# Norms at the end of a block: six layer norms on ScalarE and GpSimd, the rms scale on ScalarE, the rms norm's weights in the rows of the next projections

## The chip, the cores and the metric

The kernel runs on one core of a Trainium2 chip. The metric is the device time of one execution in microseconds. The engines are named as in the profile: PE (TensorE), DVE (VectorE), ACT (ScalarE), POOL (GpSimd) and SP, whose queue issues most DMAs.

## The reference

A sequence of 1024 tokens of width 1024 goes through a first block (layer norm, projection, an S5 state-space branch beside latent attention, a gated addition), a second block (rms norm, one wide projection, dilated attention beside a gated recurrence) and 32 experts. The change lies where the first block ends and the second begins. In the reference, in fp32:

```python
u = DEEPNORM_ALPHA * x + mix
ple = jax.nn.sigmoid(u @ w_pg[i]) * (p[i] @ w_pp[i])
x = layer_norm(u + ple, ln_g[i], ln_b[i])      # end of block 1, kept as x1
...
h = rmsnorm(x, norm1_g[layer])                 # start of block 2
z = h @ w_in[layer]                            # 3 x 512 + 4 x 512 columns
```

where `layer_norm` is (x - mean) * rsqrt(var + 1e-5) * g + b and `rmsnorm` is x * rsqrt(mean(x²) + 1e-6) * g, both over the 1024 columns.

## The kernel before

Tokens lie in 8 tiles `u[0..7]` of 128 tokens (partitions) by 1024 columns. Every fp32 product is made of three passes (`mm3`, L178 to L180): each operand is split into a rounded part h and a rest l, and PE sums h·h, h·l and l·h. A split (`split`) is one ACT operation for h (L146) and one DVE operation for l (L147).

Weights come in chunks (`Chunks`, `wload`): a chunk is 1024 rows by 256 columns, loaded in four pieces (kp 0 to 3) into `wraw` (two buffers) by SP, then split into `wh` and `wl` (eight buffers, so two chunks). `Chunks.next()` has the chunk after the present one issued as well. A piece of `wraw` comes free when its `wl` has been made.

A scheduler puts the instructions of each engine into one order when the program is built; each engine then takes its own row of instructions in that order, and waits where an operand isn't ready. That order, not the order in the code, says what stands behind a wait.

The stage in question is the last loop of `out_ple`. Per tile m, PE makes the last two quarters of the gate (60 matmuls of 256 columns), ACT takes the tanh (L695), DVE multiplies and adds it into u[m] (L696, L697). Then DVE takes the statistics and the reciprocal root (`ln_stats`, `rsqrt`: three Newton steps of small operations), applies the layer norm in two operations (L737, L738) with the gains `plg` and offsets `plb`, which are loaded as rows repeated on all partitions; SP stores the tile to `d_x1` (L739). `rms_transposed` lets ACT square and sum the tile (L751), DVE make the second root (L753 on) and scale the tile by root and gain `g1b` (L756), PE transpose it in eight 128x128 blocks (L215), and ACT and DVE evacuate and split the transposed tile into `aTh` and `aTl` (L146, L147), the operands of block 2.

Block 2 loads small constants (hmask, lb, hg), makes `lbt` on ACT (L1031), and begins its projections: `g_qk(0)` on tokens 0 to 511 (96 matmuls), `g_tok` on tiles 0 to 3 (96), `g_qk(0)` on tokens 512 to 1023 (96), `g_tok` on tiles 4 to 7 (96); after that, attention is woven between the other projections.

Of the kernel before, what the change touches and what calls it, by code (L numbers as in the profile page):

```python
# [11 lines left out]
FT = mybir.dt.float32  # L12
FR = mybir.dt.float32r
I32 = mybir.dt.int32
AF = mybir.ActivationFunctionType
OP = mybir.AluOpType
# [5 lines left out]
D = 1024  # L22
NT = 8
# [65 lines left out]
def bcast_rows(ap, n, parts=128):  # L89
    return bass.AP(tensor=ap.tensor, offset=ap.offset, ap=[[0, parts], [1, n]])  # L90


class Ctx:
# [58 lines left out]
                nc.scalar.activation(h, src, AF.Identity, scale=scale)  # L152
            nc.vector.scalar_tensor_tensor(l, src, scale, f32(h), op0=OP.mult, op1=OP.subtract)

    def wload(self, segs, nk, pj):

        nc = self.nc
        out = []
        n = sum(s.shape[1] for s in segs)
        for kp in range(nk // 2):  # L160
            raw = self.wp.tile([128, 2, WN], FT, name="wraw", bufs=2)
            o = 0
            for s in segs:
                w = s.shape[1]
                v = (s.rearrange("(p j) n -> p j n", j=nk) if pj
                     else s.rearrange("(j p) n -> p j n", p=128))
                nc.sync.dma_start(raw[:, :, o:o + w], v[:, 2 * kp:2 * kp + 2, :])
                o += w
            h = self.wp.tile([128, 2, WN], FR, name="wh")
            l = self.wp.tile([128, 2, WN], FR, name="wl")  # L170
            self.split(h[:, :, :n], l[:, :, :n], raw[:, :, :n])
            out += [(h[:, 0, :n], l[:, 0, :n]), (h[:, 1, :n], l[:, 1, :n])]
        return out

# [96 lines left out]
def block1(c):  # L271
# [111 lines left out]
    ym = [(yp.tile([128, S], FR, name=f"ymh{h}"), yp.tile([128, S], FR, name=f"yml{h}")) for h in range(4)]  # L383
    mla(c, ym, ess)
    out_ple(c, ym, esy)


# [5 lines left out]
def ln_stats(c, X):  # L393

    nc = c.nc
    n = len(X)
    mv = c.sm([128, n, 2], name="bmv")
    for i, x in enumerate(X):
        st = c.sm([128, 2, 6], name="bst")
        for h in range(2):  # L400
            nc.vector.bn_stats(st[:, h, :], x[:, h * 512:(h + 1) * 512])  # L401
        nc.vector.bn_aggr(mv[:, i], st)
    ve = c.sm([128, n], name="bve")
    nc.vector.tensor_scalar(ve, mv[:, :, 1], 1e-5, None, op0=OP.add)
    r = c.sm([128, n], name="brs")
    c.rsqrt(r, ve)
    mb = c.sm([128, n], name="bmb")
    nc.vector.scalar_tensor_tensor(mb, mv[:, :, 0], -1.0, r, op0=OP.mult, op1=OP.mult)
    return [(mv[:, i, 0:1], mb[:, i:i + 1], r[:, i:i + 1]) for i in range(n)]
# [224 lines left out]
def out_ple(c, ym, esy):  # L634
    tc, nc, I = c.tc, c.nc, c.I
# [14 lines left out]
    ch = Chunks(c, [([I["w_out"][:, s]], 8, False) for s in ns] + [([I["w_pg"][:, s]], 8, True) for s in ns])  # L650
# [10 lines left out]
    for n in range(4):  # L661
        w = ch.next()
        for m in range(NT):
# [3 lines left out]
            if n == 3:  # L667
                if m % 2 == 0:
                    uT.append(alloc_aT())
                js = slice((m % 2) * 128, (m % 2) * 128 + 128)  # L670
                c.transpose8(u[m], True, lambda q: tuple(a[:, 4 * q:4 * q + 4, js] for a in uT[m // 2]))
    esy.close()
    q = c.pool(es, "ple")
# [10 lines left out]
    def gate(m, w):  # L684
        js = slice((m % 2) * 128, (m % 2) * 128 + 128)
        psa = c.ps((128, 256))
        c.gemm(psa, [(tuple(a[:, k, js] for a in uT[m // 2]), w[k]) for k in range(8)])
        return psa

    def add(m, n, psa):  # L690
        ms = slice(m * 128, (m + 1) * 128)
        psb = c.ps((128, 256))
        c.gemm(psb, [((pTh[:, k, ms], pTl[:, k, ms]), (wph[:, k, ns[n]], wpl[:, k, ns[n]])) for k in range(2)])
        th = q.tile([128, 256], FT, name="th", bufs=2)
        nc.scalar.activation(th, psa, AF.Tanh, scale=0.5)  # L695
        nc.vector.scalar_tensor_tensor(th, th, 1.0, psb, op0=OP.add, op1=OP.mult)  # L696
        nc.vector.tensor_tensor(u[m][:, ns[n]], u[m][:, ns[n]], th, op=OP.add)  # L697
# [3 lines left out]
    for m2 in range(4):  # L701
        ps = c.psum_tile("T", [128, 2, 2, 128])
        for i in range(2):
            m = 2 * m2 + i
# [15 lines left out]
                add(m, n, gate(m, w))  # L720
    g_b = q.tile([128, D], FT, name="plg")
    b_b = q.tile([128, D], FT, name="plb")
    g1 = q.tile([128, D], FT, name="g1b")
    nc.sync.dma_start(g_b, bcast_rows(I["ln_g"], D))
    nc.sync.dma_start(b_b, bcast_rows(I["ln_b"], D))
    nc.sync.dma_start(g1, bcast_rows(I["norm1_g_2"], D))
    w = ch.next(), ch.next()
    for m in range(NT):
        add(m, 2, gate(m, w[0]))
        add(m, 3, gate(m, w[1]))  # L730
        if m % 2 == 0:
            c.hT.append(alloc_aT())
        x = u[m]
        ms = slice(m * 128, (m + 1) * 128)
        c.dbg("u_ple", x, lambda o: o[ms, :])
        (mean, _, r), = ln_stats(c, [x])
        nc.vector.scalar_tensor_tensor(x, x, mean, g_b, op0=OP.subtract, op1=OP.mult)  # L737
        nc.vector.scalar_tensor_tensor(x, x, r, b_b, op0=OP.mult, op1=OP.add)  # L738
        nc.sync.dma_start(d_x1[ms, :], x)  # L739
        c.dbg("x1", x, lambda o: o[ms, :])  # L740
        js = slice((m % 2) * 128, (m % 2) * 128 + 128)
        rms_transposed(c, q, x, [a[:, :, js] for a in c.hT[m // 2]], g1)
    es.close()


def rms_transposed(c, q, x, dst, g):

    nc = c.nc
    ss = c.sm([128, 1], name="rss")
    junk = q.tile([128, D], FT, name="junk")  # L750
    nc.scalar.activation(junk, x, AF.Square, accum_out=ss)  # L751
    v = c.sm([128, 1], name="rv")
    nc.vector.tensor_scalar(v, ss, 1.0 / D, 1e-6, op0=OP.mult, op1=OP.add)  # L753
    r = c.sm([128, 1], name="rr")
    c.rsqrt(r, v)
    nc.vector.scalar_tensor_tensor(x, x, r, g, op0=OP.mult, op1=OP.mult)  # L756
    c.transpose8(x, True, lambda h: tuple(a[:, 4 * h:4 * h + 4] for a in dst))


def s5_prep(c, es):  # L760
# [252 lines left out]
def block2(c):  # L1013

    tc, nc, I = c.tc, c.nc, c.I
# [5 lines left out]
    k = c.pool(es, "b2k")  # L1021
# [12 lines left out]
    nc.vector.tensor_scalar(fc[:, 1], th, 0.25, 0.75, op0=OP.mult, op1=OP.add)  # L1034
    nc.vector.tensor_scalar(fc[:, 2], th, 0.25, -0.25, op0=OP.mult, op1=OP.add)
    c.oss = k.tile([128, S], FT, name="oss")
    fp = c.pool(es, "b2f")
    tok = lambda kk, m: tuple(a[:, kk, (m % 2) * 128:(m % 2) * 128 + 128] for a in c.hT[m // 2])
    two = lambda kk, mm: tuple(a[:, kk, :] for a in c.hT[mm])
    bs = lambda o, b, n=1: W[:, o + b * 128:o + (b + n) * 128]  # L1040
    ft = lambda n, dt=FT: fp.tile([128, S], dt, name=n, tag="f", bufs=8)
    QK, V, G, FQ = {}, {}, {}, {}
    ch = Chunks(c, [([s], 8, True) if not isinstance(s, tuple) else (list(s), 8, True) for s in (
        (bs(0, 0), bs(512, 0)), bs(1024, 0, 2), (bs(0, 1), bs(512, 1)), (bs(0, 2), bs(512, 2)), bs(1024, 2, 2),
        (bs(0, 3), bs(512, 3)), bs(2560, 0, 2), (bs(2048, 0), bs(1536, 0)), bs(3072, 0, 2),
        (bs(2048, 1), bs(1536, 1)), bs(3072, 2, 2), (bs(2048, 2), bs(1536, 2)), bs(2560, 2, 2),
# [104 lines left out]
    r = c.con.tile([128, NT], FT, name="arr")  # L1151
# [769 lines left out]
def build(tc, I, out, dbg=None):  # L1921
    c = Ctx(tc, I, dbg)
    block1(c)
    rt = block2(c)
    c.es_ps.close()
    c.esw.close()
    moe(c, rt, out)
    c.es_ps.close()
    c.es_x2.close()
    c.es.close()  # L1930
# [37 lines left out]
```

## Time and profile before

| what | value |
|---|---|
| median of 3 runs | 2118.91 us (2117.28 to 2119.07) |
| the profiled execution's own time | 2121.21 us |
| its span | 2119.4 us, mean granted PE clock 0.954 |
| PE busy | 1937.4 us (91%) |
| DVE busy | 1549.3 us (73%) |
| ACT busy | 1031.9 us (49%) |
| POOL busy | 359.6 us (17%) |
| last loop of `out_ple` | 704.0 to 763.8 us (last gate matmul) |
| first four projection groups of block 2 | end at 827.1 us |

Times in the profile are counted from the start of the span. Busy time of PE is the time in which matmuls were in flight. A row of waits names the engine and line that waited, what it waited for, the total, the number of waits and the longest. The granted clock is 1.00 at full speed and 0.50 when PE is throttled.

### The profile page before, as it was taken

What the parts mean: (1) busy time and instruction counts of PE and PEld (TensorE: products, weight loads), DVE (VectorE), ACT (ScalarE), POOL (GpSimd) and SP (SyncE); (2) the same over time, 40 slices, a digit from 0 to 9 for tenths busy, and PEclk for the clock granted to TensorE, in tenths of its full rate; (3) what the DMA queues carried; (4) which work ended last, traced back from release to release, by engine and by line L of the source; (5) the groups of instructions that cost most, each with busy time, mean ns of one, the idle gap of its engine ahead of it and who ended that gap; (6) DMA issues with size and microseconds to landing.
All of it is one profiled execution on the core that took longest, in us unless ns stands there. A gap on an engine that the chain in (4) does not pass through costs nothing.

```text
span 2119.4 us, 34707 instructions
## 1 busy us (share of the span) xinstructions
PE 1937.4 (91%) x13274; PEld 1719.4 (81%) x13274; DVE 1549.3 (73%) x2974; ACT 1031.9 (49%) x1572; POOL 359.6 (17%) x265
## 2 busy tenths in 40 slices
PE   3997987799999979999999999999799999999992
PEld 2785875588999979899999898898688888888881
DVE  7878887777334795766457455658999999999995
ACT  3323334344222234545333223235688888888883
POOL 3124333300000000010010000003322222222211
PEclk9998998799999989999999998899899999999996
DMA  4444443311313131111111010456899999999984
GB/s 172 131 130 136 126 121 108 94 37 36 140 41 110 51 108 47 49 51 46 48 43 47 26 36 27 147 196 235 289 370 377 380 369 373 366 367 360 358 306 170
DMA packets 145081, 350.74 MB, mean 165 GB/s; under 512 B 33568, under 2 KB 87456, under 8 KB 120336
## 3 DMA queue, kind: packets, MB, share of 16 engines
q1 hardware_dynamic: 129632, 327.48, 43.0%
q0 software_dynamic: 10384, 17.87, 3.4%
q10 hardware_dynamic: 4896, 3.15, 0.7%
q8 instruction: 105, 1.72, 0.3%
q14 instruction: 64, 0.52, 0.1%
HBM read 305.81 MB, written 56.11 MB: 171 GB/s over the span
## 4 chain that ended last, share of the span: by engine, by line
PE 47%; issue 25%; DVE 14%; POOL 6%; DMA 3%; ACT 2%; SPq 1%; POOLq 0%; DVEq 0%; ACTq 0%
PE psG L178 10%; PE psG L179 10%; PE psG L180 10%; POOL gates L1824 3%; PE psT L1262 2%; PE psPO L1213 2%; PE psPO L1346 1%; POOL xg L1824 1%; PE psPO L599 1%; PE psSC L1192 1%; PE psT L215 1%; DVE wl L147 1%; PE psSC L1193 1%; DVE Sc L1332 1%; DVE bst L401 1%
## 5 line engine op out<-in xcount | busy, mean ns | idle before, releaser
L1859 DVE TENSOR_TENSOR el<-raw,eh 128x1024 fp32r<-128x1024 f32 x384 | 446.0, 1218 | 31.8 <-ACT eh L1858 31.3
L1858 ACT ACTIVATE eh<-raw 128x1024 fp32r<-128x1024 f32 x384 | 396.4, 1059 | 62.3 <-PE psUU L180 25.2
L178 PE MATMUL psG<-aTh,wh 128*128 128x256 f32 x640 | 188.6, 295 | 0.0
L179 PE MATMUL psG<-aTl,wh 128*128 128x256 f32 x640 | 184.9, 289 | 0.0
L180 PE MATMUL psG<-aTh,wl 128*128 128x256 f32 x640 | 184.9, 289 | 0.0
L146 ACT ACTIVATE wh<-wraw 128x512 fp32r<-128x512 f32 (+1 forms) x148 | 91.5, 625 | 181.4 <-PE psG L180 77.1
L147 DVE TENSOR_TENSOR wl<-wraw,wh 128x512 fp32r<-128x512 f32 (+1 forms) x148 | 107.7, 736 | 61.8 <-ACT wh L146 49.5
L178 PE MATMUL psG<-wh,aTh 128*128 128x256 f32 x512 | 147.6, 288 | 0.4 <-ACT vi L139 0.4
L179 PE MATMUL psG<-wl,aTh 128*128 128x256 f32 x512 | 146.3, 286 | 0.0
L180 PE MATMUL psG<-wh,aTl 128*128 128x256 f32 x512 | 145.5, 284 | 0.0
L178 PEld LDWEIGHTS psG<-aTh,wh 128*128 128x128 f32 x640 | 125.1, 195 | 4.8 <-issue 3.9
L180 PEld LDWEIGHTS psG<-aTh,wl 128*128 128x128 f32 x640 | 124.9, 195 | 1.9 <-issue 1.4
L179 PEld LDWEIGHTS psG<-aTl,wh 128*128 128x128 f32 x640 | 125.3, 196 | 1.4 <-issue 0.9
L178 PE MATMUL psG<-xTh,wh 128*128 128x512 f32 x256 | 102.4, 401 | 15.3 <-DVE co L326 15.1
L178 PE MATMUL psY<-eh,hh 128*128 128x512 f32 x256 | 102.3, 400 | 1.7 <-ACT hh L150 1.7
L180 PE MATMUL psG<-xTh,wl 128*128 128x512 f32 x256 | 102.0, 399 | 1.4 <-DVE wl L147 1.4
L178 PE MATMUL psUU<-eh,xh 128*128 128x512 f32 x256 | 102.6, 401 | 0.0
L178 PE MATMUL psGG<-eh,xh 128*128 128x512 f32 x256 | 101.1, 395 | 0.7 <-ACT xh L146 0.7
L179 PE MATMUL psG<-xTl,wh 128*128 128x512 f32 x256 | 101.3, 396 | 0.0
L180 PE MATMUL psGG<-eh,xl 128*128 128x512 f32 x256 | 100.9, 394 | 0.0
L178 PEld LDWEIGHTS psG<-wh,aTh 128*128 128x128 f32 x512 | 98.0, 191 | 2.9 <-issue 2.1
L179 PE MATMUL psGG<-el,xh 128*128 128x512 f32 x256 | 100.3, 392 | 0.0
(545 smaller groups left out, 5421.7 us busy)
## 6 DMA issues: line engine op xcount, KB each, us to landing
raw<-w_gate SPq DMA_DIRECT2D x64, 1024.0 KB
raw<-w_down SPq DMA_DIRECT2D x64, 1024.0 KB
raw<-w_up SPq DMA_DIRECT2D x63, 1024.0 KB
wraw<-w_in SPq DMA_DIRECT2D x52, 256.0 KB
wraw<-w_in SPq DMA_DIRECT2D x68, 128.0 KB
wraw<-w_out SPq DMA_DIRECT2D x32, 256.0 KB
x<-x SPq DMA_DIRECT2D x8, 512.0 KB
d_xln<-x SPq DMA_DIRECT2D x8, 512.0 KB
```

The costliest lines, as they stand in the source:

```text
L146: nc.scalar.activation(h, src, AF.Copy)
L147: nc.vector.tensor_sub(l, src, f32(h))
L178: mm(ps, ah, bh, start=first, stop=False)
L179: mm(ps, ah, bl, start=False, stop=False)
L180: mm(ps, al, bh, start=False, stop=last)
L215: self.nc.tensor.transpose(ps[:, i, :], src, self.ident)
L401: nc.vector.bn_stats(st[:, h, :], x[:, h * 512:(h + 1) * 512])
L1213: nc.tensor.matmul(po[64 * j:64 * j + 64], v[:, k, (b % 2) * 128 + 64 * j:(b % 2) * 128 + 64 * j + 64], et[j][:, i, :], start=k == 0, stop ...
L1262: nc.tensor.transpose(ps[:, i, :], e[:, (k0 + i) * 128:(k0 + i + 1) * 128], c.ident)
L1824: c.nc.gpsimd.indirect_dma_start(out=dst, out_offset=None, in_=src, in_offset=bass.IndirectOffsetOnAxis(ap=idx, axis=0), bounds_check=src. ...
L1858: nc.scalar.activation(h, src, AF.Copy)
L1859: nc.vector.tensor_sub(l, src, f32(h))
```

## The change

Six of the eight layer norms (tiles 0 to 5) are made as (x * r + mb) on ACT (L740), times the gain on POOL (L741) and plus the offset on POOL (L742). Tiles 6 and 7 stay on DVE (L744, L745). The rms scale of all eight tiles is an ACT operation into a new tile `xr` (L763, two buffers), which the transposes read; the square goes to the same tile (L758). The gain of the rms norm is no longer applied to the tile: it is loaded as a column tile `g1c` (one value per row of the weight matrix) in block 2, and every piece of block 2's projection weights is multiplied by it while it is split. For that the split of a piece is made in two halves, each an ACT operation with a scale (L152) and a DVE operation (L153) of 128x256. The repeated row tile `g1b` and its load go. Lines behind `wload` move by 4 (L215 becomes L219, L178 to L180 become L182 to L184), those of block 2 by 7 to 10.

```diff
-    def wload(self, segs, nk, pj):
+    def wload(self, segs, nk, pj, gains=None):
...
-            self.split(h[:, :, :n], l[:, :, :n], raw[:, :, :n])
+            if gains is None:
+                self.split(h[:, :, :n], l[:, :, :n], raw[:, :, :n])
+            else:
+                for i in range(2):
+                    self.split(h[:, i, :n], l[:, i, :n], raw[:, i, :n], scale=gains[:, 2 * kp + i:2 * kp + i + 1])
...
-    g1 = q.tile([128, D], FT, name="g1b")
...
-    nc.sync.dma_start(g1, bcast_rows(I["norm1_g_2"], D))
...
-        (mean, _, r), = ln_stats(c, [x])
-        nc.vector.scalar_tensor_tensor(x, x, mean, g_b, op0=OP.subtract, op1=OP.mult)
-        nc.vector.scalar_tensor_tensor(x, x, r, b_b, op0=OP.mult, op1=OP.add)
+        (mean, mb, r), = ln_stats(c, [x])
+        if m < NT - 2:
+            nc.scalar.activation(x, x, AF.Identity, bias=mb, scale=r)
+            nc.gpsimd.tensor_tensor(x, x, g_b, op=OP.mult)
+            nc.gpsimd.tensor_tensor(x, x, b_b, op=OP.add)
+        else:
+            nc.vector.scalar_tensor_tensor(x, x, mean, g_b, op0=OP.subtract, op1=OP.mult)
+            nc.vector.scalar_tensor_tensor(x, x, r, b_b, op0=OP.mult, op1=OP.add)
...
-    junk = q.tile([128, D], FT, name="junk")
-    nc.scalar.activation(junk, x, AF.Square, accum_out=ss)
+    xr = q.tile([128, D], FT, name="xr", bufs=2)
+    nc.scalar.activation(xr, x, AF.Square, accum_out=ss)
...
-    nc.vector.scalar_tensor_tensor(x, x, r, g, op0=OP.mult, op1=OP.mult)
-    c.transpose8(x, True, lambda h: tuple(a[:, 4 * h:4 * h + 4] for a in dst))
+    nc.scalar.activation(xr, x, AF.Identity, scale=r)
+    c.transpose8(xr, True, lambda h: tuple(a[:, 4 * h:4 * h + 4] for a in dst))
...
+    g1 = k.tile([128, 8], FT, name="g1c")
+    nc.sync.dma_start(g1, I["norm1_g_2"].rearrange("(p j) -> p j", j=8))
...
-    ch = Chunks(c, [([s], 8, True) if not isinstance(s, tuple) else (list(s), 8, True) for s in (
+    ch = Chunks(c, [(list(s) if isinstance(s, tuple) else [s], 8, True, g1) for s in (
```

The change also moves the rows of the engines. On PE, the last transposes: in the rows below psT is a transposed tile, `u5` to `u7` and `xr` the normed tiles, psG with `wh`/`wl` and `aTh`/`aTl` a projection of block 2, psG with `wph` the last matmul of the gate stage. Before, 120 matmuls of block 2's projections stand between the last gate matmul and these rows:

```order
L178 MATMUL psG_7979<-wh_7830,aTh_6701 128x256
L179 MATMUL psG_7979<-wl_7831,aTh_6701 128x256
L180 MATMUL psG_7979<-wh_7830,aTl_6702 128x256
L215 MATMUL psT_7589<-ident_68,u6_4791 128x128 x4
L215 MATMUL psT_7596<-ident_68,u6_4791 128x128 x4
L215 MATMUL psT_7727<-ident_68,u7_4792 128x128 x4
L215 MATMUL psT_7734<-ident_68,u7_4792 128x128 x4
L178 MATMUL psG_8005<-wh_7812,aTh_6701 128x256
```

And with the change, right behind the last gate matmul:

```order
L184 MATMUL psG_7668<-wph_5923,pTl_5922 128x256
L219 MATMUL psT_7453<-ident_68,xr_7431 128x128 x4
L219 MATMUL psT_7460<-ident_68,xr_7431 128x128 x4
L219 MATMUL psT_7593<-ident_68,xr_7571 128x128 x4
L219 MATMUL psT_7600<-ident_68,xr_7571 128x128 x4
L219 MATMUL psT_7731<-ident_68,xr_7709 128x128 x4
L219 MATMUL psT_7738<-ident_68,xr_7709 128x128 x4
L182 MATMUL psG_7862<-aTh_6699,wh_7788 128x256
```

The transposes of tiles 5 to 7 now stand together ahead of all of block 2's projections. Those of tiles 0 to 4 stand 108, 112, 114, 117 and 115 matmuls behind the last gate matmul of their tile (before: 118, 130, 155, 183 and 201).

On SP's queue, the loads of block 2's first chunks (`wraw` from `w_in_2`; pieces 0 and 1 of the first chunk, 7779 and 7786, stand ahead of the stores) lay between the stores of `d_x1` before:

```order
L739 DMA d_x1_4768<-u3_4788 128x1024
L167 DMA wraw_7793<-w_in_2 128x2x128 x2
L739 DMA d_x1_4768<-u4_4789 128x1024
L167 DMA wraw_7800<-w_in_2 128x2x128 x2
L167 DMA wraw_7810<-w_in_2 128x2x256
L167 DMA wraw_7816<-w_in_2 128x2x256
L167 DMA wraw_7822<-w_in_2 128x2x256
L167 DMA wraw_7828<-w_in_2 128x2x256
L739 DMA d_x1_4768<-u5_4790 128x1024
```

With the change (pieces 0 and 1 of the first chunk, 7785 and 7794, again stand ahead of the stores, 7803 and 7812 are pieces 2 and 3):

```order
L746 DMA d_x1_4768<-u6_4791 128x1024
L746 DMA d_x1_4768<-u7_4792 128x1024
L1030 DMA hmask_7766<-hmask 128x128
L1032 DMA lb_7768<-hgrn_gamma_2 128x8x1
L1034 DMA hg_7770<-hgrn_norm_g_2 128x4x1
L1046 DMA g1c_7780<-norm1_g_2 128x8
L1194 DMA alibi_8327<-alibi 128x1024
L1194 DMA alibi_8329<-alibi 128x1024
L167 DMA wraw_7803<-w_in_2 128x2x128 x2
L167 DMA wraw_7812<-w_in_2 128x2x128 x2
```

The load of g1c stands behind all eight stores, and every later piece of weights behind it. On ACT the first splits of these weights stood between the norms before:

```order
L146 ACTIVATE aTh_6979<-psT_7178 128x4x128
L146 ACTIVATE wh_7782<-wraw_7779 128x512
L146 ACTIVATE wh_7789<-wraw_7786 128x512
L695 ACTIVATE th_7635<-psG_7603 128x256
L751 ACTIVATE junk_7289,rss_7288<-u4_4789 128x1024
```

and with the change they stand behind the last tile's evacuation and behind `lbt`:

```order
L763 ACTIVATE xr_7709<-u7_4792,rr_7713 128x1024
L146 ACTIVATE aTh_7539<-psT_7731 128x4x128
L146 ACTIVATE aTh_7539<-psT_7738 128x4x128
L1038 ACTIVATE lbt_7773<-lbt_7773 128x4
L152 ACTIVATE wh_7788<-wraw_7785,g1c_7780 128x256 x2
L152 ACTIVATE wh_7797<-wraw_7794,g1c_7780 128x256 x2
L152 ACTIVATE wh_7806<-wraw_7803,g1c_7780 128x256 x2
```

So the first split with the gain moved from beside tiles 3 and 4 to behind tile 7.

More of the change, by code (lines that the diff above doesn't have):

```diff
@@ L741, in out_ple, with rms_transposed @@
         js = slice((m % 2) * 128, (m % 2) * 128 + 128)
-        rms_transposed(c, q, x, [a[:, :, js] for a in c.hT[m // 2]], g1)
+        rms_transposed(c, q, x, [a[:, :, js] for a in c.hT[m // 2]])
     es.close()
-def rms_transposed(c, q, x, dst, g):
+def rms_transposed(c, q, x, dst):
     nc = c.nc
     ss = c.sm([128, 1], name="rss")
-    junk = q.tile([128, D], FT, name="junk")
-    nc.scalar.activation(junk, x, AF.Square, accum_out=ss)
+    xr = q.tile([128, D], FT, name="xr", bufs=2)
+    nc.scalar.activation(xr, x, AF.Square, accum_out=ss)
     v = c.sm([128, 1], name="rv")
```

## The prediction

> **What bounds the kernel now.** I read the page's first table, then the stretches around the change, then who waits for whom there, and at last the chain that ended last.
>
> The first table, and one row for each stretch (start:end, length, then busy us and count of PE, PEld, DVE, ACT, POOL, then the granted clock, DMA share and GB/s):
>
> ```profile
> PE 1937.4 (91%) x13274; PEld 1719.4 (81%) x13274; DVE 1549.3 (73%) x2974; ACT 1031.9 (49%) x1572; POOL 359.6 (17%) x265
> ```
> ```profile
> 704.00:763.80 59.80, 59.15 (x497) 58.52 (x496) 55.96 (x187) 17.93 (x38) 0.00 (x0) 1.00 0.16 58
> 763.80:827.10 63.30, 51.44 (x406) 50.32 (x405) 40.39 (x110) 22.83 (x42) 0.00 (x0) 0.89 0.30 89
> 784.01:797.66 13.65, 6.57 (x30) 6.22 (x31) 11.29 (x30) 5.97 (x12) 0.00 (x0) 0.50 0.44 121
> 900.00:950.00 50.00, 50.00 (x449) 45.34 (x449) 32.23 (x77) 23.88 (x48) 4.29 (x6) 1.00 0.16 51
> ```
>
> PE is the bound nearly everywhere. The changed stage has two parts. From 704.0 to the last gate matmul at 763.8 PE is busy 59.15 of 59.80 us and DVE 55.96. From there to the end of the first four groups of block 2's projections (384 matmuls) at 827.1 PE loses 11.9 us, and 13.65 us run at clock 0.50. At 900 to 950 PE is 50.00 of 50.00, so a delay made before is not won back there. Who makes PE wait from 700 to 830 (total, times, longest), and the chain there:
>
> ```profile
> PE psT L215 <- DVE rs_b L200: 6.4, 4, 5.0
> PE psT L215 <- DVE u L756: 4.8, 1, 4.8
> PE psT L215 <- DVE rs_o L205: 0.9, 2, 0.8
> ```
> ```profile
> 786.34 1.10 PE psT L215 x4
> ...
> 791.61 1.30 DVE u L756
> 793.04 1.94 PE psT L215 x8
> ```
>
> PE's only real waits are the transposes of normed tiles 6 and 7, which it reaches before DVE has finished them; the last starts 793.04 - 763.80 = 29.2 us after the last gate. At most these 5.0 + 4.8 us, the smaller waits of 2.1 and the half clock (6.57 us of work at half speed, some 3.3 us) can be gained: 15 us.
>
> **The change, part by part.** Durations (name, form, count, then busy and mean ns):
>
> ```profile
> L756 DVE SCALAR_TENSOR_TENSOR u<-u,rr,g1b 128x1024 f32<-128x1024 f32 x8 | 10.2, 1280 | 0.5 <-DMA d_x<-u 0.5
> L738 DVE SCALAR_TENSOR_TENSOR u<-u,brs,plb 128x1024 f32<-128x1024 f32 x8 | 10.2, 1277 | 0.0
> L737 DVE SCALAR_TENSOR_TENSOR u<-u,bmv,plg 128x1024 f32<-128x1024 f32 x8 | 10.2, 1276 | 0.0
> L401 DVE BATCH_NORM_STATS2 bst<-u 128x6 f32<-128x512 f32 x13 | 8.9, 688 | 0.1
> L751 ACT ACTIVATE junk<-u 128x1024 f32<-128x1024 f32 x8 | 8.5, 1062 | 7.7 <-DVE u L738 7.7
> L697 DVE TENSOR_TENSOR u<-u,th 128x256 f32<-128x256 f32 x17 | 7.1, 420 | 0.2
> L696 DVE SCALAR_TENSOR_TENSOR th<-th,psG 128x256 f32<-128x256 f32 x17 | 7.0, 412 | 3.5 <-PE psG L180 3.5
> L695 ACT ACTIVATE th<-psG 128x256 f32<-128x256 f32 x17 | 6.5, 382 | 29.2 <-PE psG L180 28.5 <-DVE wl L147 0.7
> ```
> ```profile
> L308 POOL TENSOR_TENSOR x<-x,lng 128x1024 f32<-128x1024 f32 x8 | 21.3, 2683 | 35.0 <-ACT x L307 35.0
> L307 ACT ACTIVATE x<-x,bmb,brs 128x1024 f32<-128x1024 f32 x8 | 9.6, 1233 | 16.6 <-DVE bmb L408 16.6
> ```
> ```profile
> 789.18 0.15 DVE L753 TENSOR_SCALAR rv<-rss 128x1 f32<-128x1 f32 x1 [0.40 <-ACT junk L751]
> ...
> 791.61 1.28 DVE L756 SCALAR_TENSOR_TENSOR u<-u,rr,g1b 128x1024 f32<-128x1024 f32 x1
> ```
>
> L307 and L308 are the first layer norm, which has the operations that six of the eight tiles now get.
>
> *Removed from DVE:* 6 x (1.276 + 1.277) + 8 x 1.280 = 25.6 us. The stage has 0.65 us of PE idle before the last gate, so there this buys nothing; it can pay only after it. The 512 KB broadcast load of g1b goes; no wait stands on it: 0.
>
> *The chain of a tile gets longer.* From a tile's last gate matmul to its transposes, tiles 0 to 5 now need: tanh, product and add 0.38 + 0.41 + 0.42; the last statistics 0.69 and some 0.4 for the aggregate and small steps; a reciprocal root 2.4 (789.18 to 791.61); ACT 1.23; two POOL operations of 2.36 to 2.68 (the first is the half of the two-operation row further below); ACT's square 1.06 + 0.19; the second root 2.4; ACT's scale 1.06 to 1.23. That is 15.4 to 16.2 us with every engine free and no hand-over counted. ACT's queue holds the squares, which wait for POOL, ahead of the next tanh, and there are a dozen hand-overs: I add 1 to 3 us, so L is 16.5 to 19, and I take 17.7.
>
> *PE's order gets tighter.* A matmul takes (59.15 - 3.9)/480 = 0.115 us (480 gate matmuls and four tiles' transposes at 0.97 us, half the 1.94 above). In the built order of before, 118 to 232 matmuls stand between a tile's last gate matmul and its transposes, growing to tile 5. In the changed one 108, 112, 114, 117 and 115 matmuls stand there for tiles 0 to 4: 12.4 us for tile 0, and some 13.2 + 1.0 for each other, with the transposes of the tile before. L is longer, so PE stalls. A stall also counts into the next tile's L, so stalls pair up: s0 = L - 12.4, and s1 + s2 and s3 + s4 are L - 14.2 each. Sum 3L - 40.8: 8.7 at L = 16.5, 12.3 at 17.7, 16.2 at 19. I take 12.3. Tile 4's transposes, which stood behind the last gate, now stand ahead of it: +1.0 here.
>
> *Behind the last gate the cover goes.* Before, 120 projection matmuls stood between the last gate and tile 7's transposes, with weights that were loaded from 758.81 to 777.7 between the stores of d_x1:
>
> ```profile
> 758.81 0.90 SPq L167 DMA_DIRECT2D wraw<-w_in  x2
> ...
> 763.39 8.84 SPq L167 DMA_DIRECT2D wraw<-w_in  x6
> 773.13 0.34 SPq L739 DMA_DIRECT2D d_x<-u  x1
> 775.80 1.91 SPq L167 DMA_DIRECT2D wraw<-w_in  x4
> 781.30 6.97 SPq L739 DMA_DIRECT2D d_x<-u  x2
> ...
> 789.61 0.78 SPq L1027 DMA_DIRECT2D hg<-hgrn_norm_g  x1
> ```
>
> Now the split of every weight tile needs the column g1c. Its load is issued on SP behind all eight stores of d_x1 and behind hmask, lb and hg, and its first use stands on ACT behind tile 7's evacuation. PE has the transposes of tiles 5, 6 and 7 in a row and then the first projection matmul: nothing covers them. From the last gate: 1.2 (tanh to add), 1.1, root 2.4 beside L744 1.28, L745 1.28, square 1.25, root 2.4, scale 1.2, transposes 1.0 to 1.9, evacuation 0.6, lbt 0.2, first split 0.4: 13 us alone, and with tile 6's like work (some 5 us on the same DVE and ACT) up to 20. I take 18.5. Then 384 x 0.115 = 44.2. Only weight pairs 0 and 1 are loaded by then; pairs 2 and 3 wait for the splits of 0 and 1 to free the two raw buffers. One round:
>
> ```profile
> 816.62 3.77 DMA wraw<-w_in
> 820.47 0.63 ACT wh L146
> ```
>
> 3.8 and about 1.2 for the split, against 24 matmuls in reach (2.8 us): 2.2 open, and again up to 2 for the second chunk: I take 3 of 1 to 5. The half clock after the idle costs 1.7 (one 3.4 us stretch) to 3.3: 3. Sum 18.5 + 44.2 + 3 + 3 = 68.7 against 63.3: +5.4 (from 13 + 44.2 + 1 + 1.7 = 59.9, -3.4, to 20 + 44.2 + 5 + 3.3 = 72.5, +9.2).
>
> *Splits in halves.* 56 pairs: one 128x512 ACT operation of 0.63 becomes two of 128x256, by L695 0.38 each, +0.13; on DVE 2 x 0.42 for about 0.73, +0.1. At 900 to 950 both engines have 18 us and more free beside a full PE, which hides it; without that cover 56 x 0.13 = 7. I take 0 of 0 to 2.
>
> **Sum:** 12.3 + 1.0 + 5.4 + 0 = +18.7. The profiled run took 2121.21 us (span 2119.4), 2.3 above the median of 2118.91. 2121.21 + 18.7 = 2139.9; put on the median, 2137.6.
>
> **A rule on shared ports.** Two kinds of row bear on POOL's new work:
>
> ```profile
> 19.36 4.73 POOL L308 TENSOR_TENSOR x<-x,lng 128x1024 f32<-128x1024 f32 x2 [18.92 <-ACT x L307]
> ```
> ```profile
> 19.46 2.35 DVE L192 TENSOR_SCALAR rs_i<-bve 128x2 int32<-128x2 int32 x1
> ...
> 21.80 2.31 DVE L202 TENSOR_TENSOR rs_b<-rs_o 128x2 f32<-128x2 f32 x1
> 24.23 0.15 DVE L202 TENSOR_TENSOR rs_b<-rs_i 128x2 f32<-128x2 f32 x1
> ```
>
> A DVE operation that takes 0.15 alone took 2.3 beside POOL's, until POOL was done: DVE stands still for some 2.3 us of a POOL operation. The Trainium skill ("Trainium Architecture — The Big Picture", What this means for kernel authors) says that DVE and GpSimd share a port pair under an exclusive lock, and "Perfetto Trace Analysis" (Optimizing Scalar/DVE Operations) that moving work between those two might therefore not help; these rows agree. By it the sum has the worse end of L, rival 3.
>
> **Rivals.**
> 1. *Faster.* The wait at tiles 6 and 7 is DVE's backlog. If the freed 25.6 us let tile 7 finish 13 us behind the last gate, with the load rounds at 1 and the clock at 1.7, the tail is 3.4 shorter; it decides if L stays under 13.6, where 3L - 40.8 is nothing. For: DVE is the one named in every wait. Against: L's free sum is 15.4. With all 15 us gained: 2104; with the tail alone 2116.
> 2. *Within 0.2% (4.2 us), the change pays for itself.* L at 15.4 (stalls 5.4), the tail 3 us shorter than before, the transposes 1.0: 2122. For: the free sums. Against: 19.46 to 24 above, where DVE's small steps were far from free.
> 3. *Much slower.* DVE's lock-out puts 2.3 us on two steps of each chain: L is 21 or more, the stalls 22. And half clock after stalls:
>
> ```profile
> 333.70 0.48 PE L425 MATMUL psT<-ident,s5y 128*128 128x128 f32 x1 [2.86 <-ACT s5y L979]
> ```
> ```profile
> 333.45:336.87 3.42, 3.17 (x15) 3.17 (x16) 1.46 (x2) 2.79 (x4) 0.00 (x0) 0.50 0.41 140
> ```
>
> After 2.86 us of idle the clock was 0.50 for 3.4 us; three such stretches cost 5. 2118.9 + 22 + 1 + 5.4 + 5 = 2152.
>
> **How the numbers follow.** Forecast 0.66, rival 1 0.06, rival 2 0.10, rival 3 0.18. The predicted time is 2137. The forecast's own range, stalls 8.7 to 16.2 and tail 0 to +9.2, is 2128 to 2147. To leave out 2 in 10, the range goes from 2123, above rivals 1 and 2, to 2150, within rival 3. About 0.2% is what a measurement of this kernel tells from no change. Slower 0.84, same 0.11, faster 0.05.
>
> **What would show it.** In the trace of the changed kernel: PE waits at L219 for xr of tiles 0 to 4, 1 to 5 us each, 12 in all; the last gate some 13 us later against the stage's start; about 18 us from there to the first projection matmul, with the last PE waits on L152; PE waits for weight pairs 2 and 3; POOL 12 new operations of 2.4 to 2.9 and DVE's small steps beside them over 2 us. Beyond 900 everything is shifted by one amount. The prediction is wrong if L is under 15 (no stalls), if POOL's operations do not hold DVE up, or if something after 900 takes the delay back.

## The result: slower by about 1.2%

| | before | changed |
|---|---|---|
| median, us (4 runs each) | 2118.10 (2117.16 to 2119.07) | 2145.77 (2143.40 to 2149.10) |
| ratio, 95% interval | | 1.0122 (1.0106 to 1.0138) |
| profiled execution, us | 2121.21 | 2149.10 |
| start of the 3751st PE matmul to the end of the last gate matmul, us | 66.3 | 83.1 |
| from there to the end of the 384th projection matmul, us | 64.8 | 71.3 |

The last two rows are read from the two traces; PE runs 13274 matmuls in both, with the same instructions in the same order up to this stage, so that the 3751st is the same instruction. Together the two stretches are 23.3 of the 27.9 us that lie between the profiled executions. Another 4.9 us arise between 53 and 90 us, where both kernels have the same instructions in the same order (last section). From the 4750th to the 7000th matmul the distance of the two traces stays within 28.3 to 28.4 us, and at the end it is 27.5: nothing is won back.

The page of the changed kernel, and who makes its PE wait from 700 to 900 us:

```profile
PE 1943.3 (91%) x13274; PEld 1723.7 (80%) x13274; DVE 1543.5 (72%) x3010; ACT 1060.4 (49%) x1642; POOL 389.2 (18%) x277
```
```profile
PE psT L219 <- ACT xr L763: 27.8, 8, 6.8
PE psG L182 <- ACT wh L152: 2.1, 1, 2.1
PE psG L182 <- ACT vi L139: 0.7, 1, 0.7
```

PE waits for all eight tiles' `xr` now. Its waits for DVE are gone, and DVE is far from full in the gate stage (third pair of numbers behind the length; before it was 55.96 of 59.80):

```profile
720.00:740.00 20.00, 16.32 (x126) 16.12 (x124) 11.59 (x49) 6.81 (x12) 9.72 (x4) 0.91 0.13 53
740.00:760.00 20.00, 15.25 (x128) 14.85 (x127) 11.33 (x45) 8.93 (x14) 9.77 (x4) 1.00 0.07 27
```

No engine is full: 15 to 16 us of PE, 11 of DVE, 7 to 9 of ACT and 10 of POOL in 20 us. So the time must lie in steps that wait for each other: a ring, in which a step of one tile waits for a step of the tile before it. ACT, POOL and DVE in order of time show it (start, duration, line, and in brackets the idle time ahead and its releaser):

```profile
730.22 1.24 ACT L740 ACTIVATE u<-u,bmb,brs 128x1024 f32<-128x1024 f32 x1 [0.29 <-DVE bmb L412]
...
736.60 1.06 ACT L758 ACTIVATE xr<-u 128x1024 f32<-128x1024 f32 x1 [3.90 <-POOL u L742]
...
740.70 1.15 ACT L763 ACTIVATE xr<-u,rr 128x1024 f32<-128x1024 f32 x1 [2.67 <-DVE rr L209]
741.85 1.24 ACT L740 ACTIVATE u<-u,bmb,brs 128x1024 f32<-128x1024 f32 x1
```
```profile
731.53 2.38 POOL L741 TENSOR_TENSOR u<-u,plg 128x1024 f32<-128x1024 f32 x1 [6.69 <-ACT u L740]
734.00 2.57 POOL L742 TENSOR_TENSOR u<-u,plb 128x1024 f32<-128x1024 f32 x1
743.17 2.41 POOL L741 TENSOR_TENSOR u<-u,plg 128x1024 f32<-128x1024 f32 x1 [6.60 <-ACT u L740]
```
```profile
737.78 0.15 DVE L760 TENSOR_SCALAR rv<-rss 128x1 f32<-128x1 f32 x1 [2.74 <-ACT xr L758]
...
741.65 0.16 DVE L412 SCALAR_TENSOR_TENSOR bmb<-bmv,brs 128x1 f32<-128x1 f32 x1
```

ACT takes its row in order: layer norm (L740) of a tile, wait for POOL, square (L758), wait for DVE's root, scale (L763), and only then the layer norm of the next tile. Layer norm 1.24, POOL 5.1, square 1.15, DVE 2.95 and scale 1.15 make 11.6 us from 730.22 to 741.85, and the next two rounds take 11.6 as well. DVE closes the same ring a second time: its row starts the root of one tile (`rv`), which waits for the square, ahead of the last steps of the next tile's layer norm, so that `bmb`, which that layer norm needs, was done at 741.81, no more than 0.04 us before the scale. PE's work for a tile is some 8.05 us (60 matmuls 0.118 apart and 8 transposes in 0.97). The rest is waiting.

Behind the last gate matmul (785.1), ACT and SP's queue:

```profile
801.85 1.15 ACT L763 ACTIVATE xr<-u,rr 128x1024 f32<-128x1024 f32 x1 [2.15 <-DVE rr L209]
...
806.49 0.20 ACT L1038 ACTIVATE lbt<-lbt 128x4 f32<-128x4 f32 x1 [0.83 <-DVE lbt L1037]
806.60 1.69 ACT L152 ACTIVATE wh<-wraw,g1c 128x256 fp32r<-128x256 f32 x4
810.90 0.91 ACT L152 ACTIVATE wh<-wraw,g1c 128x256 fp32r<-128x256 f32 x2 [2.61 <-DMA wraw<-w_in]
```
```profile
724.87 73.03 SPq L746 DMA_DIRECT2D d_x<-u  x8
...
800.10 0.50 SPq L1046 DMA_DIRECT2D g1c<-norm_g  x1
...
808.03 1.92 SPq L167 DMA_DIRECT2D wraw<-w_in  x4
```

The first weights are split 21.5 us behind the last gate matmul, the first projection matmul starts at 807.1, and the next weights are only then loaded.

### The profile page after: what moved, and what is told of

The parts are those of the page before. It is cut to its first block, busy times and chain, and to the rows that moved or that the text cites. A ratio compares the mean times of both kernels' runs of the same rounds, so it can differ in the third digit from the quotient of the medians.

```text
span 2147.3 us, 34838 instructions
## 1 busy us (share of the span) xinstructions
PE 1943.3 (91%) x13274; PEld 1723.7 (80%) x13274; DVE 1543.5 (72%) x3010; ACT 1060.4 (49%) x1642; POOL 389.2 (18%) x277
## 4 chain that ended last, share of the span: by engine, by line
PE 44%; issue 28%; DVE 13%; POOL 7%; ACT 3%; DMA 3%; SPq 1%; POOLq 0%; DVEq 0%; ACTq 0%
PE psG L182 9%; PE psG L183 9%; PE psG L184 9%; POOL gates L1834 3%; PE psT L1272 2%; PE psPO L1223 2%; PE psPO L1356 1%; POOL xg L1834 1%; PE psPO L603 1%; PE psSC L1202 1%; PE psSC L1203 1%; PE psT L219 1%; DVE Sc L1342 1%; POOL u L742 1%; PE psSC L1334 1%
## 5 line engine op out<-in xcount | busy, mean ns | idle before, releaser
L182 PE MATMUL psG<-aTh,wh 128*128 128x256 f32 x640 | 188.3, 295 | 2.1 <-ACT wh L152 2.1
L184 PE MATMUL psG<-aTh,wl 128*128 128x256 f32 x640 | 184.6, 289 | 0.0
L182 PE MATMUL psG<-wh,aTh 128*128 128x256 f32 x512 | 148.0, 289 | 0.7 <-ACT vi L139 0.7
L184 PE MATMUL psG<-wh,aTl 128*128 128x256 f32 x512 | 145.8, 285 | 0.0
L182 PEld LDWEIGHTS psG<-aTh,wh 128*128 128x128 f32 x640 | 125.0, 195 | 7.2 <-issue 3.9
L184 PEld LDWEIGHTS psG<-aTh,wl 128*128 128x128 f32 x640 | 124.6, 195 | 1.9 <-issue 1.4
L146 ACT ACTIVATE wh<-wraw 128x512 fp32r<-128x512 f32 x92 | 56.3, 620 | 138.0 <-PE psG L184 76.8
L182 PE MATMUL psG<-xTh,wh 128*128 128x512 f32 x256 | 104.0, 408 | 15.3 <-DVE co L330 15.1
L184 PE MATMUL psG<-xTh,wl 128*128 128x512 f32 x256 | 103.6, 405 | 1.6 <-DVE wl L147 1.5
L182 PE MATMUL psY<-eh,hh 128*128 128x512 f32 x256 | 102.3, 400 | 1.7 <-ACT hh L150 1.7
L182 PE MATMUL psUU<-eh,xh 128*128 128x512 f32 x256 | 102.6, 401 | 0.0
L182 PE MATMUL psGG<-eh,xh 128*128 128x512 f32 x256 | 100.9, 394 | 0.7 <-ACT xh L146 0.7
L182 PEld LDWEIGHTS psG<-wh,aTh 128*128 128x128 f32 x512 | 98.5, 192 | 3.3 <-issue 2.1
L183 PE MATMUL psY<-el,hh 128*128 128x512 f32 x256 | 100.3, 392 | 0.4 <-DVE el L1869 0.4
L184 PE MATMUL psGG<-eh,xl 128*128 128x512 f32 x256 | 100.4, 392 | 0.0
L184 PE MATMUL psY<-eh,hl 128*128 128x512 f32 x256 | 100.2, 391 | 0.0
```

Of the source, the lines that this page charges most:

```text
L146: nc.scalar.activation(h, src, AF.Copy)
L182: mm(ps, ah, bh, start=first, stop=False)
L183: mm(ps, ah, bl, start=False, stop=False)
L184: mm(ps, al, bh, start=False, stop=last)
```

## The experiments

All medians stand beside runs of the kernel before on the same chip. "Gate part" and "tail" are the two stretches of the table above.

| run | gate part | tail | sum less before's 131.1 | ratio to before (95%) |
|---|---|---|---|---|
| changed | 83.1 | 71.3 | +23.3 | 1.0122 (1.0106 to 1.0138) |
| e1 column early | 83.1 | 57.7 | +9.7 | 1.0066 (1.0046 to 1.0086) |
| e2 norms on DVE | 67.4 | 68.3 | +4.6 | 1.0035 (1.0021 to 1.0049) |
| e3 both | 67.7 | 54.2 | -9.2 | 0.9981 (0.9970 to 0.9992) |
| e4 no POOL steps | 70.1 | 66.5 | +5.5 | 1.0036 (1.0022 to 1.0050) |
| e5 both, padded | 67.2 | 54.3 | -9.6 | 0.9958 (0.9942 to 0.9974) |
| e6 before, shifted | 66.7 | 67.4 | +3.0 | 1.0016 (1.0002 to 1.0030) |
| e7 transposes later | 78.8 | 62.7 | +10.3 | 1.0042 (1.0027 to 1.0056) |
| e8 layer norms alone | 79.7 | 73.8 | +22.4 | 1.0109 (1.0084 to 1.0133) |
| e9 ring opened | 77.5 | 62.4 | +8.8 | 1.0040 (1.0023 to 1.0056) |
| e10 ring, one tile | 78.5 | 56.2 | +3.6 | 1.0010 (0.9994 to 1.0025) |
| e11 one POOL step | 74.0 | 75.9 | +18.8 | 1.0094 (1.0067 to 1.0120) |

### e1: the column early

```diff
+    c.g1c = c.con.tile([128, 8], FT, name="g1c")          # ahead of the last loop of out_ple
+    nc.sync.dma_start(c.g1c, I["norm1_g_2"].rearrange("(p j) -> p j", j=8))
...
-    g1 = k.tile([128, 8], FT, name="g1c")                 # in block2
+    g1 = c.g1c
```

> The changed kernel, with the column g1c loaded into the pool of constants ahead of the last loop of out_ple instead of in block 2. Theory A (the loss behind the last gate comes from the late load, which puts every projection behind tile 7): 114 matmuls (13.3 us) now stand between the last gate and tile 7's transposes; these were ready 18 us after the last gate, so PE waits some 4 us, and the stretch from the last gate to the end of the first four projection groups falls from 70 us to 50 to 55, the stalls ahead of the last gate stay at 13: 2122 to 2127 us. Theory B (the loss behind the last gate is the price of the halved splits and of ACT's longer queue): the stretch stays near 70 us: about 2141.

2136.75 us (before beside it: 2122.95). PE's waits for xr fell from 27.8 us to

```profile
PE psT L219 <- ACT xr L765: 16.2, 7, 3.7
```

of which 12.3 us are the five ahead of the last gate, as before this edit. The tail fell by 13.6 us to 57.7, to 7 under the kernel before: the late load, with the order of rows that follows from it, was its whole loss. The total missed my range by more than the chip's offset, since the tail came out 3 to 8 us longer than expected and, as e5 and e6 show, the new 32 bytes themselves cost time.

### e2: all layer norms on DVE

```diff
-        if m < NT - 2:
+        if m < NT - 8:
```

> The changed kernel with all eight layer norms on DVE (no POOL operation), the rms scale on ACT and the column g1c late as in the change. Theory A (POOL and ACT make the chain longer than the matmuls that PE has in between): the chain is some 12 us against 117 to 130 matmuls (13.7 to 15 us), the five stalls ahead of the last gate fall from 13 us to under 3, while behind the last gate the three tiles' transposes still stand ahead of all projections, 68 to 74 us to the end of the fourth group: 2126 to 2132. Theory C (the stalls follow from PE's tighter order alone, whoever makes the norms): they stay at 8 to 13 us: 2137 or more.

2130.09 us (2122.95 beside it). The five waits ahead of the last gate are gone; what is left lies behind it:

```profile
PE psT L219 <- ACT xr L763: 12.1, 4, 6.4
PE psG L182 <- ACT wh L152: 2.1, 1, 2.1
```

So the gate part's loss comes from the norms on ACT and POOL. The tail's mostly does not: it is 68.3, against 71.3 in the changed kernel and 64.8 before.

### e3: both

The edits of e1 and e2 together.

> Both: layer norms on DVE and the column loaded early; what is left of the change is the rms scale on ACT and the gain in the weights. Theory A: no stalls ahead of the last gate, and 114 matmuls cover behind it: 2106 to 2113, faster than before. Rival: DVE's backlog returns (it loses only 8 x 1.28 us against before), tile 7's transposes come 25 us or more behind the last gate as before: 2114 to 2119.

2120.89 us (2122.95 beside it): faster, by 2 us instead of the expected 5 or more. The rival does not hold either: tile 7's transposes come 18.8 us behind the last gate, not 25 or more. In the stage the two edits add up: e1 takes 13.6 us off the changed kernel's sum and e2 18.7, and both together 32.5. But behind 830 us the trace lost some 4 us of its lead over the kernel before again, bit by bit.

### e4: without POOL's steps

```diff
-            nc.gpsimd.tensor_tensor(x, x, g_b, op=OP.mult)
-            nc.gpsimd.tensor_tensor(x, x, b_b, op=OP.add)
```

> The changed kernel without the two POOL operations of tiles 0 to 5 (gain and offset of these layer norms are left out; ACT's normalization stays). If POOL's two operations are the part of the chain that is too long: the chain falls by 4.9 us to 11.5 to 14, against 98 to 102 matmuls (11.5 us) and the transposes; the five stalls fall from 13 us to 0 to 4, the stretch behind the last gate stays near 70: 2125 to 2131. If it is ACT's queue or the hand-overs: stalls of 8 us or more, 2134 or more.

This kernel leaves out the gain and offset of six layer norms. 2131.01 us (2122.95 beside it). One wait of 0.7 us and smaller ones are left ahead of the last gate, though PE has only 98 to 102 matmuls in between. ACT still has the layer norm, the square and the scale of each tile: POOL's two steps are what made the rest too long.

### e5 and e6: where the operands lie

e5 is e3 with a column tile of 64 bytes instead of 32. e6 is the kernel before with an unused tile of 32 bytes:

```diff
+    nc.vector.memset(c.con.tile([128, 8], FT, name="gap"), 0.0)
```

> As the run with the layer norms on DVE and the column early, but the column takes 64 instead of 32 bytes of each partition. In that run every later tile lay 32 bytes further on, 256-column matmuls began 119.9 ns apart instead of 117.5 to 118.3, and some 4 us were lost bit by bit behind 830 us. Theory D (the place of the operands, a multiple of 32 but not of 64 bytes, slows the matmuls): the spacing is back at 117.5 to 118.3, the loss behind 830 goes, 8 to 11 us faster than before in all. Rival (the loss is the halved splits or the earlier weights): the spacing stays near 119.9, and no more than 3 to 6 us faster.

> The kernel before with an unused tile of 32 bytes in the pool of constants ahead of the last loop of out_ple, nothing else. Theory D: the spacing of 256-column matmuls from 700 us on rises from 117.5 to 118.3 to about 119.9 ns, and the kernel is 4 to 8 us slower than before. Rival: no change of the spacing, and the same time within 2 us.

e5: 2115.42 us (2124.78 beside it), e6: 2128.70. One row each of e3 and e5, 15 us in which PE does nothing but these projections (the number in brackets behind PE's busy time counts its matmuls):

```profile
795.00:810.00 15.00, 15.00 (x127) 15.00 (x126) 4.36 (x8) 3.74 (x8) 0.00 (x0) 1.00 0.01 1
```
```profile
795.00:810.00 15.00, 15.00 (x130) 15.00 (x129) 4.10 (x8) 4.12 (x9) 0.00 (x0) 1.00 0.04 12
```

127 matmuls against 130. In the gate part the mean distance of two starts is 118.3 ns before, 119.9 in e3 and e6, 117.3 in e5. e6's trace loses 6.6 us between the 3750th and the 13250th matmul by nothing but the shift, so the place of the operands is shown as the cause; its ratio, 1.0016, is smaller than those 6.6 us would make it. e5 is the fastest version.

### e7: the transposes later

The changed norms, the column early and padded, and the transposes of a tile written three tiles later:

```diff
+        late.append(rms_transposed(c, q, x, ...))     # returns its transposes
+        if m >= 3:
+            late[m - 3]()
```

> The change with its norms on ACT and POOL, the column early and padded to 64 bytes, xr with four buffers, and each tile's transposes written three tiles later: 180 matmuls (21 us) stand between a tile's last gate matmul and its transposes instead of 108 to 117. Theory A (the stalls are the chain of 16 to 19 us less the matmuls in between): no stalls over 1 us ahead of the last gate; behind it tile 7's chain of 18 us has 94 matmuls (11 us) as cover, one wait of 5 to 8 us; together 3 to 8 us faster than before. Rival (POOL's hold on DVE and the longer ACT queue cost PE time whatever the order): stalls of 5 us or more ahead of the last gate, and slower than before by 5 or more.

2132.15 us (2124.78 beside it). The rival was right that time is lost whatever the order; of the two reasons it gave, the rows show ACT's. With 180 matmuls of cover the two stretches lose 10.3 us, against 9.7 in e1, whose column is early too: 4 us less ahead of the last gate, 5 more behind it. Ahead of it PE's waits have another name:

```profile
PE psG L182 <- ACT th L699: 12.1, 9, 1.6
PE psT L219 <- ACT xr L771: 6.9, 2, 6.5
```

The waits for xr ahead of the last gate are gone (the 6.9 lie behind it), and nine waits for ACT's tanh have come: the tanh, which frees the gate's PSUM tile, stands behind the square that waits for POOL. POOL's first operations still start 11.0 to 11.7 us apart. So the pace of the ring doesn't depend on the cover; the cover moves a part of the loss behind the last gate.

### e8: the layer norms alone

The kernel before with `if m < NT - 2` and ACT and POOL's layer norm; the rms part untouched.

> One part of the change alone: six layer norms on ACT and POOL; the rms scale with g1b on DVE as before, no gains in the weights. 111, 122, 151, 176 and 196 matmuls stand between gate and transposes of tiles 0 to 4, and 120 behind the last gate ahead of tile 7's. Theory A: stalls of 4 us at tile 0 and 0 to 3 at tile 1, none at 2 to 4; DVE is 15 us freer, so tile 7's transposes wait 3 to 6 us less than the 10 before: within 4 us of before. Rival (the norms on POOL cost time whatever stands between): 10 us or more slower.

2147.69 us (2124.78 beside it): nearly the whole loss, against my expectation and as the rival had it. ACT shows a ring that is longer still:

```profile
731.22 1.23 ACT L738 ACTIVATE u<-u,bmb,brs 128x1024 f32<-128x1024 f32 x1
...
737.48 1.06 ACT L756 ACTIVATE junk<-u 128x1024 f32<-128x1024 f32 x1 [4.75 <-POOL u L740]
...
743.27 1.09 ACT L146 ACTIVATE aTh<-psT 128x512 fp32r<-128x512 f32 x2 [3.21 <-PE psT L215]
...
745.54 1.24 ACT L738 ACTIVATE u<-u,bmb,brs 128x1024 f32<-128x1024 f32 x1 [1.18 <-DVE bmb L408]
```

Here DVE's root and scale and PE's transposes lie in the ring as well. On ACT the next layer norm stands behind the evacuation of the tile's transposes, and then it waits 1.18 us more for DVE, where `bmb` (745.35) stands behind the split of the same transposes (L147, 743.97 to 745.24). This round takes 14.3 us, the one behind it 15.2, the ones around them 13.5 and 13.1. The tail is 9.0 us longer than before, though no column is waited for: behind the last gate PE's waits for DVE grew from 12.1 to 15.5 us, and the rest isn't explained.

### e9, e10 and e11: other rings

e9 writes the whole rms part of a tile two tiles later, e10 one tile later (both with norms on ACT and POOL, column early and padded); e11 is the changed kernel with the offset added on DVE.

```diff
-        rms_transposed(c, q, x, ...)
+        if m >= 2:                      # e10: m >= 1
+            rms(m - 2)                  # rms_transposed of that tile
```
```diff
-            nc.gpsimd.tensor_tensor(x, x, b_b, op=OP.add)        # e11
+            nc.vector.tensor_add(x, x, b_b)
```

> As the run with later transposes (norms of tiles 0 to 5 on ACT and POOL, column early and padded, 180 matmuls of cover), but the whole rms part of a tile, square and scale too, is written two tiles later, so that on ACT the layer norm of tile m + 1 stands ahead of the scale of tile m, and of the square of tile m no longer behind the scale of m - 1. Theory E (a ring through ACT's row sets the pace: layer norm on ACT 1.24, POOL 4.9, square 1.24, root 3.0, scale 1.15, and only then the next layer norm, 11.6 us a tile against 8.05 of PE): the ring shrinks to 1.24 + 4.9 + 1.24 = 7.4, POOL's first operations start 8.0 to 8.6 us apart instead of 11.6, PE's waits for tanh vanish, and from 697 to 832 us it is 4 to 9 us faster than before; 2 to 8 us faster in all. Rival (POOL's hold on DVE sets the pace): POOL's starts stay 11 us or more apart, and it stays 5 us or more slower than before.

> The same with the rms part written one tile later: 120 to 130 matmuls of cover, 94 behind the last gate. Theory E: the ring is open here too, POOL's starts 8 to 9.5 us apart; the chain of some 17 to 19 us is longer than the 14 to 16 us of cover, so two or three stalls of 1 to 3 us remain: between the same time as before and 8 us slower. Rival (cover alone decides, the ring doesn't matter): stalls of 10 us or more ahead of the last gate as in the changed kernel with its 108 to 117.

> The changed kernel with the offset of tiles 0 to 5 added on DVE instead of POOL, the column late as in the change. 114, 127, 131, 157 and 178 matmuls of cover. Theory E: the ring is 1.24 + 2.4 + 1.2 to 2.4 on DVE + 1.24 + 3.0 + 1.15 = 10.2 to 11.4 us a tile, so POOL's starts are that far apart in spite of the cover, and PE loses 9 to 16 us ahead of the last gate, and 7 behind it as the change does: 14 to 22 us slower than before. Rival (stalls are the chain less the cover): with 15 us of chain against 13.4 to 21 of cover under 4 us of stalls, 8 to 12 us slower in all.

2130.06, 2126.18 and 2143.30 us (2121.95 beside them). e9, which was to be 2 to 8 us faster, is 0.4% slower. Two of its first POOL operations of a tile and two rows of its DVE:

```profile
743.66 2.37 POOL L747 TENSOR_TENSOR u<-u,plg 128x1024 f32<-128x1024 f32 x1 [5.85 <-ACT u L746]
...
754.22 2.37 POOL L747 TENSOR_TENSOR u<-u,plg 128x1024 f32<-128x1024 f32 x1 [5.65 <-ACT u L746]
```
```profile
749.79 0.15 DVE L768 TENSOR_SCALAR rv<-rss 128x1 f32<-128x1 f32 x1 [1.45 <-ACT xr L766]
...
752.71 0.15 DVE L412 SCALAR_TENSOR_TENSOR bmb<-bmv,brs 128x1 f32<-128x1 f32 x1
```

10.6 us apart in these rows, 9.2 to 10.8 over all tiles, instead of 11.6: the scale (1.15) had left the ring, and no more. On DVE the first step of the rms root (`rv`, which waits for the square) stands ahead of the last steps of the next tile's layer norm (to `bmb`), so the ring closes through DVE: POOL and square until 749.79, 3.1 on DVE, layer norm 1.24, POOL again. My 7.4 left that out, although the changed kernel's own rows show it. e10 has the same pace (10.1 to 10.7) and a shorter tail. In e11 the total came out as expected, 21 us, and so did the pace:

```profile
716.64 2.42 POOL L741 TENSOR_TENSOR u<-u,plg 128x1024 f32<-128x1024 f32 x1 [217.40 <-ACT u L740]
727.21 2.38 POOL L741 TENSOR_TENSOR u<-u,plg 128x1024 f32<-128x1024 f32 x1 [8.15 <-ACT u L740]
738.81 2.41 POOL L741 TENSOR_TENSOR u<-u,plg 128x1024 f32<-128x1024 f32 x1 [9.23 <-ACT u L740]
```

10.6 and 11.6 us apart, 10.3 to 12.4 over all tiles, although up to 178 matmuls stand between. But the loss did not lie where I expected it: 7.7 us ahead of the last gate instead of 9 to 16, and 11.1 behind it instead of 7. That is the cover at work again, as in e7. A kernel whose ring is open on DVE too wasn't tried.

## Why the prediction was right, and where not

**Direction, place and range: right.** The loss is where it was put, in PE's waits for xr ahead of the last gate and in the cover lost behind it. 2145.77 lies between 2123 and 2150, but nearer the upper end than the 2137 named.

**Stalls ahead of the last gate, 12.3: measured 13.0** (3.7, 1.7, 3.1, 3.0 and 1.6), **for a reason that was only half right.** The step was "chain L less the matmuls in between", 3L - 40.8. The first stall is of that kind: tile 0's chain took 16.45 us from its last gate matmul to its transposes, close to the 16.5 to 19 allowed. But those of tiles 1 to 4 took 20.2 to 21.3 with the stalls inside them, and with L = 16.45 the formula gives 8.6, not 13.0. So the agreement of 12.3 and 13.0 is partly luck. By that step, too, e7 should have had no stalls and e8 hardly any. What sets the pace is the ring through the in-order rows of ACT and DVE, 11.6 us a tile against some 8.05. I had listed its members and had even said that the squares wait for POOL ahead of the next tanh; I added them up as the latency of one tile and didn't ask when the next tile's first step could start.

**0.115 us a matmul: too little.** The row of 704.0 to 763.8 was taken to hold 480 gate matmuls; its 497 are 458 gate matmuls, 32 transposes and 7 projection matmuls. The loop's 480 run from 701.2 to 763.2, and two starts lie 0.118 us apart. By that the cover of the three terms is longer, which takes some 1.1 us off the stalls, and the 384 matmuls of the tail take some 1.3 us more: the sum hardly moves.

**Half clock ahead of the last gate: left out of the sum, held to be rival 3's.** It is there, 0.91 in the row of 720 to 740 above and again from 760 to 780. Each row stands for some 3.6 us at half speed, so the two cost 3.6 us at most. With tile 4's transposes (+1.0) and the waits (13.0) this is enough for the gate part's +16.8, for which the sum had 13.3.

**Tail, +5.4: measured +6.5.** The first projection started 22.05 us behind the last gate matmul against the 18.5 taken, over the 20 that were given as the bound; the waits for weights were smaller than the 3 taken. e1 confirms that the load order is the cause of the tail's loss.

**Splits in halves, 0:** right. The two traces keep their distance within 0.1 us from the 4750th to the 7000th matmul.

**Sum 18.7 against 23.3.** What lies between 23.3 and the 27.9 of the profiled executions is the early part, which no step named.

**The shared-ports rule and rival 3.** POOL's operations took 2.38 to 2.57 us, near the 2.36 to 2.68 taken, and the root lay in the ring with 2.95 against 2.4. DVE's addition (L701, 0.42 alone) was once held to 1.39 and four times to some 0.6, and none of these lies in the ring's chain of waits; no step took 2.3. So the rule did not decide here. Its hold was seen elsewhere (last section). The prediction had named two signs here: POOL did hold DVE up, but by no more than 1.0 us a tile and outside the ring, and the small steps of over 2 us did not come. Rival 3's price, 2152, is nearer to 2145.77 than the named 2137, by 6 us against 9, but its lock-out isn't what the rows show.

**Rival 1** had a true core, which the change hid. e5 keeps only the scale on ACT and the gains in the weights, takes 8 x 1.28 us from DVE, and is 0.42% faster; tile 7's transposes start 18.9 us behind the last gate there, against 29.8 before. That the shorter DVE work alone does this isn't shown, since e5 has other rows, other loads and no half clock behind the last gate as well.

## What to carry to other kernels

When work moves from one engine to three, write down for each in-order engine what the next tile's first step stands behind, and add up the ring on each of them; the longest is the pace, whatever lies between the ends. Engines that all idle a part of the time point to one. A small load that many later steps need belongs ahead of the queue that it would otherwise stand behind. And look at where a new small tile pushes the others.

## What was not expected of the hardware

**32 bytes.** Weights' tiles that begin 32 bytes off a multiple of 64 (the first `wh` at byte 25824 of its partition in e3 and e6, at 25792 before, at 25856 in e5) went with 256-column matmuls that start 119.9 ns apart instead of 117.3 to 118.3. Every other tile that lies behind the new one moved too, so it isn't shown which of them does it; the transposed tokens (`aTh`, `aTl`) lie 32 bytes off a multiple of 64 in all of these kernels.

**A race of 0.13 us, and 5 us that go with it.** Between 53 and 90 us, with the same instructions in the same order, the traces of these kernels fall into two groups: level with the kernel before within 0.5 us at the 250th matmul (e1, e2, e9, e10, e11), or 4.2 to 5.1 us later (the changed kernel and e3 to e8, and so e6, which is the kernel before but for an unused tile). First the kernel before, then the changed one, each with DVE's addition and POOL's last multiplication of the first layer norm:

```profile
53.32 1.21 DVE L309 TENSOR_TENSOR x<-x,lnb 128x1024 f32<-128x1024 f32 x1
```
```profile
53.97 2.80 POOL L308 TENSOR_TENSOR x<-x,lng 128x1024 f32<-128x1024 f32 x1 [1.72 <-ACT x L307]
```
```profile
53.49 3.38 DVE L313 TENSOR_TENSOR x<-x,lnb 128x1024 f32<-128x1024 f32 x1
```
```profile
53.36 2.43 POOL L312 TENSOR_TENSOR x<-x,lng 128x1024 f32<-128x1024 f32 x1 [0.94 <-ACT x L311]
```

Whichever starts first holds the other up: POOL loses 0.4 us, or DVE 2.2. The Trainium skill ("SBUF — State Buffer", SBUF: two separate sides) describes this as an exclusive lock on the port pair that the two share, held for a whole instruction; these rows agree: DVE's held addition ends 1.08 us behind POOL's operation, near the 1.21 that it takes alone. The order is the same within each group: in the six level traces DVE starts first, by 0.2 to 0.7 us, in the seven later ones POOL does, by 0.13 or 0.14. That the 2.2 us grow to 4 or 5 by what hangs on them is argued, not shown. The runs of the kernel before spread further, from 2117.5 to 2130.9 beside e5; how much of that is this race no trace shows. So comparisons here rest on the intervals and on stretches of the trace, not on single times.
